# A token-parallel MLP in two passes of half the tokens, its up projection by Strassen's seven products

## The chip, the core and the metric

One core of one Trainium2 chip runs the whole inference step. The metric is the device time of one execution in microseconds (us). The kernel before takes 1367.91 us in the median of three runs (1366.85 to 1371.48).

A core has five engines that run their own instruction streams and wait for each other by semaphores: TensorE (PE; matmuls, with PEld its weight loads), VectorE (DVE), ScalarE (ACT), GpSimd (POOL) and SyncE (SP, which issues DMAs). An engine runs its instructions in order: one that waits holds up all that stand behind it.

## The reference

The step is one layer of a hybrid decoder on 1032 tokens (1024 of a prompt and 8 of single-token sequences), model width 1024:

```
h    = rmsnorm(x, g1);  proj = h @ w_in
mix  = concat(pool_mixer(proj), rwkv7_mixer(proj)) @ w_out
x    = x + mix
h2   = rmsnorm(x, norm2_g)                       # x * rsqrt(mean(x*x) + eps) * g
x    = x + square(relu(h2 @ w_up)) @ w_down      # w_up 1024 x 4096, w_down 4096 x 1024
y    = rmsnorm(x, norm_f_g)
```

All of it is float32. The change touches the last three lines, and through the order of the streams the end of the line before.

## The kernel before

A float32 product is made of three fp32r matmuls. Each operand is split into a high part h, rounded to fp32r by ScalarE, and a low part l = x - h, taken by VectorE; `gemm` (line 169) then sums h·h, h·l and l·h in PSUM. Activations lie with channels on the partitions and tokens along the free axis, so that a matmul has 128x128 weights and streams up to 512 tokens. The weights are streamed from HBM in blocks of 128x512: `weights` (line 147) loads one by GpSimd's queue into wr (four buffers) and splits it into wh and wl (six each).

The tokens have three blocks: block 0 with 512, blocks 1 and 2 with 260 each. Half 0 is block 0 and half 1 is blocks 1 and 2 (520 tokens). x, the residual stream, lies in two tiles x10 and x11, loaded by `open_x1` (line 835), into which all later results are added.

Stages: the input projections, interleaved with the mixers by a table of letters (to about 560 us); the output projection of half 0 (mx of 512 columns), then of half 1 (mx of 260 columns): `mixed` (line 842) loads a piece of the mixer's output from DRAM into mr (three buffers, SyncE's queue) and splits it into mh and ml, `out_block` adds the product to x. Half 1's is in the pool `opb` (lines 915 to 927). The norm's sums of squares follow (`norm2`), and h2h and h2l are the split of x times the gain; the reciprocal root rs2 is applied after the product, in line 910.

The MLP runs over 32 feature blocks f of 128 rows of the hidden layer. `ups_of(f)` makes one: 8 k-blocks x 3 matmuls for each of the three token blocks, then line 910 (relu and rs2), 911 (square), the rounding and 913 (low part). After four feature blocks `down(g, m, b)` (line 944) adds their share of the second product to x: for each of 8 output blocks m and each token block 12 matmuls, into one of two PSUM buffers (ps_d), and one VectorE addition (line 949). Three of the four feature blocks that a group needs are made after the group before. The last group (g = 7) runs block by block and interleaves the final norm; `final` (line 966) writes the result.

The instructions' order on each engine follows from the program text, and the pools' memory: a tile that lies where an earlier pool lay is first written when the earlier one's readers are through. DMAs of one queue are issued in the order in which they stand on its engine.

Of the kernel before, what the change touches and what calls it, by code (L numbers as in the profile page):

```python
# [84 lines left out]
def _build(ctx, nc, tc, I, O, dbg):  # L85
# [793 lines left out]
    def square_sum(ps, m, c, n, acc, sq):

        act(sq if m else acc, x1s(m, c, n), AF.Square)
        if m:
            V.tensor_tensor(acc, acc, sq, op=ALU.add)
        if m == KT - 1:
            PE.matmul(ps[:, :n], ON, acc, start=True, stop=True)

    def norm2(c, n, tmp):

        for m in range(KT):
            x, h, g = x1s(m, c, n), h2[0][:, m, c:c + n], col(V_G2, m)  # L890
            act(h, x, scale=g)
            V.scalar_tensor_tensor(h2[1][:, m, c:c + n], x, g, f32(h), ALU.mult, ALU.subtract)  # L892
# [8 lines left out]
    def up(f, w, b):
        if f not in ups:
            ups[f] = [mp.tile([P, T], F32R, tag=f"u{x}", name=f"u{x}{f}", bufs=6) for x in "hl"]
        uh, ul = ups[f]
        c, n = BLK[b]
        cs = slice(c, c + n)
        ps = ps_u.tile([P, 512], F32, tag="u", name=f"up{f}_{c}")
        gemm(ps[:, :n], w, [(h2[0][:, k, cs], h2[1][:, k, cs]) for k in range(KT)])
        u = tmp(f"u{f}_{c}")[:, :n]
        V.scalar_tensor_tensor(u, ps[:, :n], 0.0, rs2[:, cs], ALU.max, ALU.mult)  # L910
        V.tensor_tensor(u, u, u, op=ALU.mult)  # L911
        act(uh[:, cs], u)
        V.tensor_tensor(ul[:, cs], u, f32(uh[:, cs]), op=ALU.subtract)
# [17 lines left out]
    tmp = lambda x, t="u": mp.tile([P, 512], F32, tag=t, name=x, bufs=3 if t == "u" else 1)  # L931
    w = weights(I["w_up"][0])
    up(0, w, 0)
    for c, n in BLK[1:]:
        norm2(c, n, tmp)
    for b in (1, 2):
        up(0, w, b)

    def ups_of(f):
        w = weights(I["w_up"][f])  # L940
        for b in range(3):
            up(f, w, b)

    def down(g, m, b, w):
        c, n = BLK[b]
        ps = ps_d.tile([P, 512], F32, tag="d", name=f"dn{g}_{m}_{b}")
        gemm(ps[:, :n], w, [(ups[4 * g + j][0][:, c:c + n], ups[4 * g + j][1][:, c:c + n]) for j in range(4)])
# [3 lines left out]
    for f in range(1, 4):
        ups_of(f)
    for g in range(7):
        ups_of(4 * g + 4)
        for m in range(KT):
            w = weights(I["w_down"][g, m])
            for b in range(3):
                down(g, m, b, w)
        for f in range(4 * g + 5, 4 * g + 8):
            ups_of(f)  # L960


    w7 = [hq.tile([P, 8, 512], F32R, tag=f"h2{x}", name=f"w7{x}") for x in "hl"]
    ws = [weights(I["w_down"][7, m], None if m < 4 else [x[:, m, :] for x in w7]) for m in range(KT)]
    pending = []
# [102 lines left out]
```

## Time and profile before

| | |
|---|---|
| median of 3 runs | 1367.91 us (1366.85 to 1371.48) |
| profiled execution | 1369.13 us, span 1367.4 us |
| mean granted TensorE clock | 0.987 |
| PE busy | 1306.5 us, 96% of the span, 9844 matmuls |
| DVE / ACT / POOL busy | 829.6 / 592.7 / 156.5 us (61%, 43%, 11%) |
| HBM read / written | 79.67 / 13.78 MB |

The span is the time from the first to the last instruction; the profiled execution's own time is 1.7 us longer. The share of an engine is an average over stages that differ: the mixers' stage up to 560 us keeps VectorE and ScalarE busy, the MLP behind it hardly. The granted clock is that of TensorE; 1.00 is 2.4 GHz and 0.50 is 1.2 GHz.

### The profile page before, as it was taken

The numbers are of one execution on the slowest core, as the hardware profiler recorded it, in microseconds if no ns is written. First come the engines' busy times: TensorE is split into PE (matmuls) and PEld (weight loads), VectorE is DVE, ScalarE is ACT, GpSimd is POOL, SyncE is SP. The second block draws the span as 40 slices with busy tenths as digits, with TensorE's granted clock in tenths as the row PEclk, the third lists the DMA queues.
The fourth block names the chain that finished last, engine by engine and source line by source line (L and its number), as shares of the span: only waits on it lengthen the run. The fifth ranks groups of instructions, "written<-read, shape, count | busy, mean of one in ns | idle before, by whom it ended". The sixth has DMA issues, their size and how long they took to land.

```text
span 1367.4 us, 24591 instructions
## 1 busy us (share of the span) xinstructions
PE 1306.5 (96%) x9844; PEld 1158.8 (85%) x9844; DVE 829.6 (61%) x1832; ACT 592.7 (43%) x1466; POOL 156.5 (11%) x306
## 2 busy tenths in 40 slices
PE   5999999999999999999999999999999999999996
PEld 5987778788777777798999999999999999999986
DVE  8887677778778656748644435445444354453447
ACT  7768777877777758526211212112111121121123
POOL 4101000210010021120010100100000100000000
PEclk9999999899999989999999999999999999999998
DMA  6323123222221244531111111111111111111103
GB/s 199 97 55 89 39 47 83 100 96 54 59 63 42 67 152 147 167 125 59 47 54 39 55 47 39 55 40 47 55 40 54 47 46 48 45 48 48 47 7 124
DMA packets 75315, 94.82 MB, mean 69 GB/s; under 512 B 46168, under 2 KB 52440, under 8 KB 75192
## 3 DMA queue, kind: packets, MB, share of 16 engines
q0 software_dynamic: 20480, 66.04, 15.1%
q1 hardware_dynamic: 53392, 25.36, 7.1%
q10 hardware_dynamic: 1328, 1.85, 0.4%
q8 instruction: 77, 1.26, 0.4%
q14 instruction: 38, 0.31, 0.1%
HBM read 79.67 MB, written 13.78 MB: 68 GB/s over the span
## 4 chain that ended last, share of the span: by engine, by line
PE 75%; ACT 9%; DVE 9%; DMA 3%; issue 2%; POOL 1%; SPq 0%; DVEq 0%; POOLq 0%; ACTq 0%
PE dn L175 26%; PE up L175 26%; PE pj L175 7%; PE mx L175 5%; ACT SV L92 2%; DVE tm L496 1%; PE sc L403 1%; PE pcs L580 1%; ACT Es L92 1%; ACT TT L92 1%; PE pcs L577 1%; DVE SV L589 1%; ACT wh L92 1%; PE pcs L573 1%; PE bkt L417 1%
## 5 line engine op out<-in xcount | busy, mean ns | idle before, releaser
L92 ACT ACTIVATE wh<-wr 128x512 fp32r<-128x512 f32 x230 | 143.8, 626 | 353.4 <-PE dn L175 276.2
L175 PE MATMUL up<-h2h,wl 128*128 128x260 f32 (+1 forms) x768 | 245.8, 320 | 0.0
L175 PE MATMUL up<-h2h,wh 128*128 128x260 f32 (+1 forms) x768 | 245.2, 320 | 0.5 <-DVE u L910 0.5
L175 PE MATMUL up<-h2l,wh 128*128 128x260 f32 (+1 forms) x768 | 245.0, 320 | 0.0
L175 PE MATMUL dn<-uh,wl 128*128 128x512 f32 (+1 forms) x720 | 231.2, 321 | 0.0
L175 PE MATMUL dn<-ul,wh 128*128 128x512 f32 (+1 forms) x720 | 230.8, 321 | 0.0
L175 PE MATMUL dn<-uh,wh 128*128 128x512 f32 (+1 forms) x720 | 230.5, 320 | 0.0
L949 DVE TENSOR_TENSOR x<-dn,x 128x260 f32<-128x260 f32 (+1 forms) x192 | 99.1, 516 | 189.8 <-PE dn L175 189.8
L175 PE MATMUL pj<-xh,wh 128*128 128x256 f32 (+1 forms) x576 | 175.3, 304 | 13.9 <-ACT wh L92 13.7
L165 DVE TENSOR_TENSOR wl<-wr,wh 128x512 fp32r<-128x512 f32 x230 | 156.5, 684 | 44.6 <-ACT wh L92 37.8
L175 PE MATMUL pj<-xh,wl 128*128 128x256 f32 (+1 forms) x576 | 171.0, 297 | 0.2 <-DVE wl L165 0.2
L175 PE MATMUL pj<-xl,wh 128*128 128x256 f32 (+1 forms) x576 | 170.5, 296 | 0.0
L175 PEld LDWEIGHTS up<-h2l,wh 128*128 128x128 f32 x768 | 144.6, 188 | 12.1 <-DVE h2l L892 0.4
L175 PEld LDWEIGHTS up<-h2h,wh 128*128 128x128 f32 x768 | 144.3, 188 | 11.6 <-DVE u L910 0.9
L175 PEld LDWEIGHTS up<-h2h,wl 128*128 128x128 f32 x768 | 144.6, 188 | 11.0
L92 ACT ACTIVATE uh<-u 128x260 fp32r<-128x260 f32 (+1 forms) x96 | 47.2, 492 | 238.6 <-DVE u L911 238.6
L175 PEld LDWEIGHTS dn<-ul,wh 128*128 128x128 f32 x720 | 135.6, 188 | 10.9 <-issue 0.2
L175 PEld LDWEIGHTS dn<-uh,wh 128*128 128x128 f32 x720 | 135.8, 189 | 10.4
L175 PEld LDWEIGHTS dn<-uh,wl 128*128 128x128 f32 x720 | 135.5, 188 | 10.6 <-issue 0.2
L175 PEld LDWEIGHTS pj<-xh,wh 128*128 128x128 f32 x576 | 111.4, 193 | 17.4 <-ACT wh L92 13.7
L910 DVE SCALAR_TENSOR_TENSOR u<-up,rs 128x260 f32<-128x260 f32 (+1 forms) x96 | 49.5, 517 | 120.9 <-PE up L175 114.3
L175 PEld LDWEIGHTS pj<-xl,wh 128*128 128x128 f32 x576 | 111.2, 193 | 2.4 <-issue 1.9
(295 smaller groups left out, 2224.3 us busy)
## 6 DMA issues: line engine op xcount, KB each, us to landing
wr<-in_w_in POOLq DMA_DIRECT2D x72, 256.0 KB, 3.1
wr<-in_w_up POOLq DMA_DIRECT2D x64, 256.0 KB, 2.8
wr<-in_w_down POOLq DMA_DIRECT2D x64, 256.0 KB, 2.9
wr<-in_w_out POOLq DMA_DIRECT2D x26, 256.0 KB, 3.1
xr<-in_xT SPq DMA_DIRECT2D x16, 256.0 KB, 3.7
mr<-mix SPq DMA_DIRECT2D x8, 260.0 KB, 3.5
x<-in_xT SPq DMA_DIRECT2D x2, 1040.0 KB, 9.1
blk<-AA SPq DMA_DIRECT2D x16, 128.0 KB, 3.3
```

Of the source, the lines that this page charges most:

```text
L92: A.activation(out, in_, func, bias=bias, scale=scale, **k)
L165: V.tensor_tensor(l[:, :w], raw[:, :w], f32(h[:, :w]), op=ALU.subtract)
L175: PE.matmul(ps, lhs, rhs, start=i == 0, stop=i == n - 1)
L403: PE.matmul(psc[:, c, :], BK[:, c, 2 * h:2 * h + 2, :], AR[:, c, :, h, :], start=True, stop=True)
L417: PE.transpose(pt[:, c, :], BK[:, c, 2 * h:2 * h + 2, :].rearrange("p a t -> p (a t)"), ident)
L496: V.tensor_tensor(pr[:, q], l[:, q].unsqueeze(2).to_broadcast([64, m, m, m]), r[:, q].rearrange("p k j -> p j k").unsqueeze(1).to_broadcas ...
L573: PE.matmul(pq, AR[:, c, 0, :, :], SV[:, c, :, :], start=True, stop=True)
L577: PE.matmul(pa, TT[:, g, :, :], Q, start=True, stop=True)
L580: PE.matmul(pu, BKT[:, c, :, :], SV[:, c, :, :], start=True, stop=True)
L589: V.scalar_tensor_tensor(dst, pu[R[h], h, :], U.gam[R[h], g:g + 1], sg[R[h], h, :], ALU.mult, ALU.add)
L910: V.scalar_tensor_tensor(u, ps[:, :n], 0.0, rs2[:, cs], ALU.max, ALU.mult)
L949: V.tensor_tensor(d, ps[:, :n], d, op=ALU.add)
```

## The change

The MLP runs in two passes: all 32 feature blocks of half 0, then all of half 1. In each pass the up projection takes the feature blocks in pairs, and a pair's product (256 features x 1024 channels by 1024 channels x 512 or 520 tokens) is cut into quarters: two feature blocks, two halves of the channels, two quarters of the tokens (q = 256 or 260). Of the eight products of quarters, Strassen's scheme (in Winograd's form) makes seven, of sums and differences of quarters:

- `up_operands(half)` makes the seven token operands x11, xt2, x21, xt3, xt1, x22, xt4: for each of four k-blocks four normed quarters b11 to b22 (x times gain times rs2, so that the norm is applied ahead of the product), four differences, and the split of seven. That is 60 VectorE and 28 ScalarE instructions a half. Its tiles have one buffer each (x11 two), so half 1's overwrite half 0's.
- `up_pair(p)`, p = 0 to 31, loads the four weight quarters a11 to a22 (128x512, SyncE's queue, one buffer each), makes four sums s1 to s4 on GpSimd, splits seven operands, and runs 7 products of 12 matmuls of q columns, b0 to b6; seven VectorE sums put the four results together, and `emit` does relu, square and rounding on ScalarE and the low part on VectorE.
- w_up and w_down are read twice; w_down's blocks come by SyncE's queue instead of GpSimd's.
- A down group of half 0 has 8 blocks of 512 columns, of half 1 8 x 2 of 260. The order on TensorE is pair 0, 1, 2, group 0, pair 3, 4, group 1, and so on; `up_operands(1)` stands ahead of group 7 of half 0, pair 16 and 17 behind it, then block 0's final norm.

The core of the diff:

```diff
-    def weights(src, into=None):
+    def weights(src, into=None, q=GP):
...
-                GP.dma_start(raw[:, :w], src[:, o:o + w])
+                q.dma_start(raw[:, :w], src[:, o:o + w])
...
+    def split(raw):
+
+        h = wp.tile([P, 512], F32R, tag="wh", name="wh", bufs=NWH)
+        l = wp.tile([P, 512], F32R, tag="wl", name="wl", bufs=NWH)
+        act(h, raw)
+        V.tensor_tensor(l, raw, f32(h), op=ALU.subtract)
+        return h, l
...
+    def up_operands(half):
+
+        c0, n = HALF[half]
+        q = n // 2
+        for i in KIND:
+            XO[half][i] = [hq.tile([P, 4, 260], F32R, tag=f"x{i}{x}", name=f"x{i}{x}{half}", bufs=NXO[i]) for x in "hl"]
...
+        for k in range(4):
+            b = {}
+            for i, (kk, o) in {"11": (k, c0), "12": (k, c0 + q), "22": (k + 4, c0 + q), "21": (k + 4, c0)}.items():
+                b[i] = xtmp(f"b{i}_{k}_{half}", q)
+                V.scalar_tensor_tensor(b[i], x1s(kk, o, q), col(V_G2, kk), rs2[:, o:o + q], ALU.mult, ALU.mult)
+            for out, x, y in (("t1", "12", "11"), ("t2", "22", "t1"), ("t3", "22", "12"), ("t4", "21", "t2")):
+                b[out] = b["12"] if out == "t3" else xtmp(f"{out}_{k}_{half}", q)
+                V.tensor_tensor(b[out], b[x], b[y], op=ALU.subtract)
+            for i in KIND:
+                put(i, k, b[i])
...
+    def up_pair(p):
+
+        half, f0 = p // 16, 2 * (p % 16)
+        q = HALF[half][1] // 2
+        X = XO[half]
...
+                a[i] = mp.tile([P, 512], F32, tag=f"a{i}", name=f"a{i}_{p}")
+                SY.dma_start(a[i], I["w_up"][f0 + f][:, 512 * k:512 * k + 512])
+        for out, x, y, op in (("s3", "11", "21", ALU.subtract), ("s1", "21", "22", ALU.add), ("s2", "s1", "11", ALU.subtract),
+                              ("s4", "12", "s2", ALU.subtract)):
+            a[out] = mp.tile([P, 512], F32, tag=f"a{out}", name=f"a{out}_{p}")
+            GP.tensor_tensor(a[out], a[x], a[y], op=op)
...
+        def product(s, x):
+            i = next(banks)
+            ps = (ps_u if i % 3 else ps_m).tile([P, 512], F32, tag="u" if i % 3 else "m", name=f"b{i}_{p}")[:, :q]
+            h, l = split(a[s])
+            for k in range(4):
+                c = slice(P * k, P * k + P)
+                xh, xl = (t[:, k, :q] for t in X[x])
+                for i, (lhs, rhs) in enumerate(((h, xh), (h, xl), (l, xh))):
+                    PE.matmul(ps, lhs[:, c], rhs, start=k == i == 0, stop=k == 3 and i == 2)
+            return ps
...
+        ps = product("11", "11")
+        p1 = tmp("p1")
+        act(p1, ps)
+        u2 = plus("u2", p1, product("s2", "t2"))
+        emit(0, 0, plus("c11", p1, product("12", "21")))
+        u3 = plus("u3", u2, product("s3", "t3"))
+        ps = product("s1", "t1")
+        u4 = plus("u4", u2, ps)
+        emit(1, 1, plus("c22", u3, ps))
+        emit(1, 0, plus("c21", u3, product("22", "t4")))
+        emit(0, 1, plus("c12", u4, product("s4", "22")))
...
         norm2(0, 512, lambda x: op.tile([P, 512], F32, tag="n2", name=x, bufs=2))
+        up_operands(0)
...
+    up_pair(0)
+    for c, n in BLK[1:]:
+        norm2(c, n, tmp)
+    up_pair(1)
+    for G in range(15):
+        half, g = G // 8, G % 8
+        if G != 7:
+            up_pair(2 * G + 2)
+        else:
+            up_operands(1)
+        for m in range(KT):
+            w = weights(I["w_down"][g, m], q=SY)
+            for blk in MB[half]:
+                down(g, m, blk, w)
+        if G == 7:
+            up_pair(2 * G + 2)
+        up_pair(2 * G + 3)
```

How the order of the streams stands before and after is shown at three places. The first is SyncE's queue at the output projection of half 1; x11 is half 1's residual tile, mr its mixer pieces. Before:

```order
L698 DMA mix7_1_85<-da_6384 128x8
L849 DMA mr0_1_7148<-mix0_1_71 128x520
L849 DMA mr1_1_7154<-mix1_1_73 128x520
L849 DMA mr2_1_7160<-mix2_1_75 128x520
L849 DMA mr3_1_7166<-mix3_1_77 128x520
L849 DMA mr4_1_7172<-mix4_1_79 128x520
L849 DMA mr5_1_7178<-mix5_1_81 128x520
L849 DMA mr6_1_7184<-mix6_1_83 128x520
L849 DMA mr7_1_7703<-mix7_1_85 128x520
L835 DMA x11_7127<-in_xT 128x4x520 x2
```

And now, with the first loads of the MLP behind them:

```order
L709 DMA mix7_1_85<-da_6384 128x8
L846 DMA x11_7127<-in_xT 128x4x520 x2
L860 DMA mr0_1_7146<-mix0_1_71 128x520
L860 DMA mr1_1_7152<-mix1_1_73 128x520
L860 DMA mr2_1_7158<-mix2_1_75 128x520
L860 DMA mr3_1_7164<-mix3_1_77 128x520
L860 DMA mr4_1_7170<-mix4_1_79 128x520
L860 DMA mr5_1_7176<-mix5_1_81 128x520
L860 DMA mr6_1_7182<-mix6_1_83 128x520
L860 DMA mr7_1_7815<-mix7_1_85 128x520
```

The two loads of x11, which wait for half 0's last matmul in both kernels, stand ahead of the eight mr loads now.

The second is VectorE at a change from ups to a down group, group 4 of half 0 (dn4_0 is its first block, wl the low part of a weight block, u and ul those of the hidden layer). Before:

```order
L165 TENSOR_TENSOR wl_11818<-wr_11815,wh_11817 128x512
L910 SCALAR_TENSOR_TENSOR u20_772_11618<-up20_772_11593,rs2_7141 128x260
L911 TENSOR_TENSOR u20_772_11618<-u20_772_11618 128x260
L165 TENSOR_TENSOR wl_11866<-wr_11863,wh_11865 128x512
L913 TENSOR_TENSOR ul20_11532<-u20_772_11618,uh20_11531 128x260
L949 TENSOR_TENSOR x10_6590<-dn4_0_0_11629,x10_6590 128x512
L949 TENSOR_TENSOR x11_7127<-dn4_0_1_11643,x11_7127 128x260
```

And now (wr_10628 is the group's fifth block, c21 and c12 are a pair's last two results):

```order
L168 TENSOR_TENSOR wl_10611<-wr_10608,wh_10610 128x512
L974 TENSOR_TENSOR c21_10_10517<-u3_10_10472,b5_10_10500 128x256
L168 TENSOR_TENSOR wl_10631<-wr_10628,wh_10630 128x512
L970 TENSOR_TENSOR ul21_10376<-u11_10_10495,uh21_10375 128x256
L974 TENSOR_TENSOR c12_10_10541<-u4_10_10491,b6_10_10524 128x256
L168 TENSOR_TENSOR wl_10651<-wr_10648,wh_10650 128x512
L970 TENSOR_TENSOR ul21_10376<-u10_10_10519,uh21_10375 128x256
L970 TENSOR_TENSOR ul20_10374<-u01_10_10543,uh20_10373 128x256
L1016 TENSOR_TENSOR x10_6590<-dn4_0_0_10554,x10_6590 128x512
L168 TENSOR_TENSOR wl_10671<-wr_10668,wh_10670 128x512
L1016 TENSOR_TENSOR x10_6590<-dn4_1_0_10574,x10_6590 128x512
```

The low parts of six of the group's blocks now stand ahead of its first addition; on SyncE the load of wr_10628 stands behind the loads of the next pair and the first of the one after:

```order
L160 DMA wr_10608<-in_w_down 128x512
L942 DMA a11_10_10377<-in_w_up 128x512
L942 DMA a12_10_10381<-in_w_up 128x512
L942 DMA a22_10_10383<-in_w_up 128x512
L942 DMA a21_11_10714<-in_w_up 128x512
L942 DMA a11_11_10712<-in_w_up 128x512
L942 DMA a12_11_10716<-in_w_up 128x512
L942 DMA a22_11_10718<-in_w_up 128x512
L942 DMA a21_12_10889<-in_w_up 128x512
L160 DMA wr_10628<-in_w_down 128x512
```

Before, these loads were on GpSimd's queue in the order of their use.

The third is VectorE at the change from half 0 to half 1 (l1 ends the name of an operand of half 1, dn7_0 is the first block of half 0's last group). Before, the same addition stands among the low parts of u and the final norm; now:

```order
L924 TENSOR_TENSOR t4_3_1_12017<-b21_3_1_12010,t2_3_1_12014 128x260
L915 TENSOR_TENSOR xt2l1_11906<-t2_3_1_12014,xt2h1_11905 128x260
L915 TENSOR_TENSOR x21l1_11908<-b21_3_1_12010,x21h1_11907 128x260
L915 TENSOR_TENSOR xt3l1_11910<-b12_3_1_12006,xt3h1_11909 128x260
L915 TENSOR_TENSOR xt1l1_11912<-t1_3_1_12012,xt1h1_11911 128x260
L915 TENSOR_TENSOR x22l1_11914<-b22_3_1_12008,x22h1_11913 128x260
L915 TENSOR_TENSOR xt4l1_11916<-t4_3_1_12017,xt4h1_11915 128x260
L1016 TENSOR_TENSOR x10_6590<-dn7_0_0_12039,x10_6590 128x512
L1016 TENSOR_TENSOR x10_6590<-dn7_1_0_12059,x10_6590 128x512
```

The last operands of half 1 stand ahead of the first addition of the group.

## Rows read from the trace of the kernel before

**Rows 1.** Busy time by stretches: us, busy PE, PEld, DVE, ACT, POOL, clock, DMA, GB/s
```profile
700.00:900.00 200.00, 200.00 (x1275) 181.52 (x1275) 90.25 (x166) 34.47 (x60) 18.80 (x35) 1.00 0.15 47
1100.00:1300.00 200.00, 200.00 (x1271) 181.26 (x1270) 92.78 (x172) 36.92 (x65) 19.35 (x36) 1.00 0.16 48
```

**Rows 2.** Timeline of PE in a down group: start us, us, engine, line
```profile
800.16 0.28 PE L175 MATMUL dn<-uh,wh 128*128 128x260 f32 x1
...
802.93 0.28 PE L175 MATMUL dn<-uh,wl 128*128 128x260 f32 x1
803.05 0.39 PE L175 MATMUL dn<-uh,wh 128*128 128x512 f32 x1
...
805.59 0.39 PE L175 MATMUL dn<-uh,wl 128*128 128x512 f32 x1
```

**Rows 3.** Timeline of PE in an input projection
```profile
289.13 0.28 PE L175 MATMUL pj<-xh,wh 128*128 128x256 f32 x1
...
291.87 0.28 PE L175 MATMUL pj<-xh,wl 128*128 128x256 f32 x1
```

**Rows 4.** Timeline of DVE in the output projection of half 1
```profile
587.58 0.69 DVE L165 TENSOR_TENSOR wl<-wr,wh 128x512 fp32r<-128x512 f32 x1 [1.54 <-ACT wh L92]
588.18 0.42 DVE L860 TENSOR_TENSOR x<-mx,x 128x260 f32<-128x260 f32 x1
588.54 0.56 DVE L165 TENSOR_TENSOR wl<-wr,wh 128x384 fp32r<-128x384 f32 x1
```

**Rows 5.** Groups of instructions from 640 us on: count, busy us and mean ns, idle before
```profile
L92 ACT ACTIVATE wh<-wr 128x512 fp32r<-128x512 f32 x117 | 74.1, 633 | 300.7 <-PE dn L175 276.2 <-PE up L175 24.2
...
L971 DVE SCALAR_TENSOR_TENSOR x<-x,vec,rs 128x512 f32<-128x512 f32 x8 | 5.8, 746 | 0.0
```

**Rows 6.** Timeline of SP's issues at the output projection
```profile
563.14 11.22 SPq L849 DMA_DIRECT2D mr<-mix  x8
574.40 0.98 SPq L835 DMA_DIRECT2D x<-in_xT  x2
```

**Rows 7.** DMA issues of the page: count, KB each, us to landing
```profile
wr<-in_w_down POOLq DMA_DIRECT2D x64, 256.0 KB, 2.9
...
xr<-in_xT SPq DMA_DIRECT2D x16, 256.0 KB, 3.7
mr<-mix SPq DMA_DIRECT2D x8, 260.0 KB, 3.5
...
glu<-in_g_lora_up SPq DMA_DIRECT2D x1, 256.0 KB, 8.9
```

**Rows 8.** Tile x, 574 to 590 us: its two loads from issue to landing
```profile
DMA to landing us min/median/max: 7.9/9.1/10.4
```

**Rows 9.** The chain that ended last, half 1's output projection: start us, us
```profile
582.77 35.42 PE mx L175 x294
```

**Rows 10.** Timeline of PE at the MLP's start, in brackets the idle time before
```profile
646.02 0.70 PE L885 MATMUL ss<-acc,cst 128*128 128x260 f32 x2 [0.74 <-DVE acc L883]
647.25 0.39 PE L175 MATMUL up<-h2h,wh 128*128 128x260 f32 x1 [0.52 <-DVE u L910]
```

**Rows 11.** Groups of instructions on POOL
```profile
L434 POOL MEMSET RB<- 128x512 f32 x4 | 1.9, 522 | 0.0
```

**Rows 12.** Timeline of PE, two matmuls behind a gap (its us in brackets)
```profile
244.92 0.80 PE L577 MATMUL pcs<-Q,TT 128*128 128x128 f32 x2 [2.90 <-ACT Q L92]
...
582.77 0.39 PE L175 MATMUL mx<-mh,wh 128*128 128x260 f32 x1 [2.37 <-DVE x L860]
```

**Rows 13.** Stretches behind three gaps, as in rows 1 (clock ahead of the DMA share)
```profile
245.00:251.00 6.00, 6.00 (x21) 5.31 (x22) 2.82 (x7) 4.67 (x14) 3.22 (x6) 0.50 0.60 201
490.00:500.90 10.90, 10.90 (x90) 7.98 (x88) 6.22 (x11) 5.54 (x14) 2.13 (x4) 0.53 0.41 137
583.00:587.00 4.00, 4.00 (x35) 4.00 (x35) 2.24 (x5) 0.72 (x2) 0.54 (x1) 1.00 0.62 221
```

More of the change, by code (lines that the diff above doesn't have):

```diff
@@ L38 @@
 NX = 2
+NXT = 8
+NUT = 10
+NXO = {"11": 2, "t2": 1, "21": 1, "t3": 1, "t1": 1, "22": 1, "t4": 1}
 QUEUE = 1
@@ L875, in _build @@
     hq = open_pool(ctx, "h2", reuse_waits="tile")
-    h2 = [hq.tile([P, KT, T], F32R, tag=f"h2{x}", name=f"h2{x}") for x in "hl"]
+    KIND = ("11", "t2", "21", "t3", "t1", "22", "t4")
+    XO = [{}, {}]
     rs2 = hq.tile([P, T], F32, name="rs2")
[L879 to L885, printed above, removed]
+    xtmp = lambda x, n: hq.tile([P, 260], F32, tag="xt", name=x, bufs=NXT)[:, :n]
     def norm2(c, n, tmp):
[L889 to L892, printed above, removed]
         ss = ps_m.tile([P, 512], F32, tag="m", name=f"ss2{c}")
@@ L895, in norm2 @@
         for m in range(KT):
-            square_sum(ss, m, c, n, acc, m and tmp(f"sq2_{c}_{m}")[:, :n])
-        rstd(rs2[:, c:c + n], ss[:, :n], tmp(f"ms2{c}")[:, :n], tmp(f"tt2{c}")[:, :n])
-    ups = {}
[L901 to L913, printed above, removed]
+            sq = tmp(f"sq2_{c}_{m}")[:, :n] if m else acc
@@ new lines, in norm2, with put @@
+            act(sq, x1s(m, c, n), AF.Square)
+            if m:
+                V.tensor_tensor(acc, acc, sq, op=ALU.add)
+        PE.matmul(ss[:, :n], ON, acc, start=True, stop=True)
+        rstd(rs2[:, c:c + n], ss[:, :n], tmp(f"ms2{c}")[:, :n], tmp(f"tt2{c}")[:, :n])
+    def up_operands(half):
[3 more added lines that the diff above has]
+            XO[half][i] = [hq.tile([P, 4, 260], F32R, tag=f"x{i}{x}", name=f"x{i}{x}{half}", bufs=NXO[i]) for x in "hl"]
+        def put(i, k, x):
+            h, l = (t[:, k, :q] for t in XO[half][i])
+            act(h, x)
+            V.tensor_tensor(l, x, f32(h), op=ALU.subtract)
+        for k in range(4):
[8 more added lines that the diff above has]
+                put(i, k, b[i])
@@ L930, in _build, with down @@
     mp = open_pool(ctx, "mlp", reuse_waits="tile")
[L931 to L947, printed above, removed]
+    tmp = lambda x, t="u": mp.tile([P, 512], F32, tag="v" + t, name=x, bufs=2 if t == "u" else 1)
+    MB = [[BLK[0]], BLK[1:]]
+    def down(g, m, blk, w):
+        c, n = blk
+        half = int(c > 0)
+        o = c - 512 * half
+        ps = ps_d.tile([P, 512], F32, tag="d", name=f"dn{g}_{m}_{c}")
+        gemm(ps[:, :n], w, [tuple(t[:, o:o + n] for t in ups[32 * half + 4 * g + j]) for j in range(4)])
         d = x1s(m, c, n)
         V.tensor_tensor(d, ps[:, :n], d, op=ALU.add)
[L951 to L965, printed above, removed]
     def final(b, m, rs):
@@ L975, in final, with final_scale @@
             (A if m == 3 else SY).dma_start(O["yT"][:, m + 1 - k:m + 1, c:c + n], x1[h][:, m + 1 - k:m + 1, o:o + n])
-    for b, (c, n) in enumerate(BLK):
+    def final_scale(b, ss):
+        c, n = BLK[b]
+        rs = mp.tile([P, 512], F32, tag="rs3", name=f"rs3{b}", bufs=2)[:, :n]
+        rstd(rs, ss[:, :n], tmp(f"ms3{b}")[:, :n], tmp(f"tt3{b}")[:, :n])
+        return [(b, m, rs) for m in range(KT)]
+    up_pair(0)
[15 more added lines that the diff above has]
+        up_pair(2 * G + 3)
+        if G == 7:
+            c, n = BLK[0]
+            ss = ps_m.tile([P, 512], F32, tag="m", name="ss30")
+            acc = tmp("acc30", "acc")
+            for m in range(KT):
+                sq = tmp(f"sq3_0_{m}") if m else acc
+                act(sq, x1s(m, c, n), AF.Square)
+                if m:
+                    V.tensor_tensor(acc, acc, sq, op=ALU.add)
+            PE.matmul(ss, ON, acc, start=True, stop=True)
+            for x in final_scale(0, ss):
+                final(*x)
+    w7 = [[hq.tile([P, 4, 260], F32R, tag=f"x{i}{x}", name=f"w7{i}{x}", bufs=NXO[i]).rearrange("p k t -> p (k t)")[:, :512]
+           for x in "hl"] for i in KIND[:4]]
+    ws = [weights(I["w_down"][7, m], None if m < 4 else w7[m - 4], q=SY) for m in range(KT)]
+    pending = []
+    for b in (1, 2):
+        c, n = BLK[b]
         ss = ps_u.tile([P, 512], F32, tag="u", name=f"ss3{b}")
@@ L980, in _build @@
         for m in range(KT):
-            down(7, m, b, ws[m])
+            down(7, m, BLK[b], ws[m])
             d = x1s(m, c, n)
@@ L994, in _build @@
             pending = []
-        rs = mp.tile([P, 512], F32, tag="rs3", name=f"rs3{b}", bufs=2)[:, :n]
-        rstd(rs, ss[:, :n], tmp(f"ms3{b}")[:, :n], tmp(f"tt3{b}")[:, :n])
-        pending += [(b, m, rs) for m in range(KT)]
+        pending += final_scale(b, ss)
     for q in pending:
```

22 lines of the change are left out of this document (21 added, 1 removed).

## The prediction

> **What bounds the kernel now.** I read the table of busy time by stretches first, since the page's shares mix the mixer's many small stages with the MLP. From 700 to 1300 us TensorE is busy in every microsecond at the full granted clock, while VectorE stands at 45% and the rings carry 47 to 48 GB/s [rows 1]: the MLP is bound by TensorE's columns and nothing else. A change that takes matmuls away there gains their pace in full, and a change that makes TensorE wait pays in full too. The second view was the timeline, for the pace from start to start (the busy time of a matmul overlaps the next one's): eleven steps of 128x512 from 803.05 to 805.59 give 0.231 us each, 23 steps of 128x260 from 800.16 to 802.93 give 0.120 [rows 2], 23 steps of 128x256 from 289.13 to 291.87 give 0.119 [rows 3].
>
> **The matmuls.** Before, the up projection is 32 x (24 x 0.231 + 48 x 0.120) = 362 us. After, it is 32 pairs of 7 products of 12 matmuls: 1344 of 256 columns and 1344 of 260, 1344 x (0.119 + 0.120) = 322 us. That is -40.4 us. The down projection has the same matmuls in another order. That seven eighths are paid for is certain; the question is what else TensorE now waits for. A pair lasts 84 x 0.119 = 10.0 us, a down group of half 0 (8 blocks of 12 matmuls of 512 columns) 96 x 0.231 = 22.2 us, so a period of two pairs and a group is 42.2 us in half 0 and 43.3 in half 1.
>
> **Bulk work beside it.** VectorE's paces are 0.60 for 128x512 (587.58 to 588.18) and 0.36 or less for 128x260 (588.18 to 588.54) [rows 4]; I use 0.61 and 0.35. Per pair: 7 lower parts of weights, 7 sums, 4 lower parts of u: 7 x 0.61 + 11 x 0.35 = 8.1 us; a down group adds 8 lower parts and 8 additions, 9.8 us; together 26 of 42.2. ScalarE, by busy means [rows 5], is lower still. So neither becomes the bound on average. The second reading of both weights adds 33.5 MB over about 700 us, 48 GB/s, where the rings are 15% busy [rows 1]: nothing by itself. The 64 more splits of w_down are in the 26.
>
> **Places where TensorE waits.**
>
> 1, out-projection of half 1. Before, SyncE issues the eight mr loads from 563.14 on, and the two loads of x for half 1 behind them at 574.40 [rows 6], when half 0's last matmul lets them. After, the order has x first and the mr loads behind. The x loads take 7.9 and 10.4 us to land [rows 8], an mr load 3.5 [rows 7]; behind 2 MB on the same queue, mr0 lands at about 586, and with three buffers for eight loads, each to be rounded and subtracted before the next is issued, the seventh is split at about 597. The matmuls that began at 582.77 [rows 9] begin at 597.5: +14.7. If the rings serve both loads side by side it is +7; if every mr load takes its 3.5 behind the other, +18. I take 14.7, since a 256 KB load behind others on this queue took 8.9 [rows 7]. The 35.4 us of matmuls behind [rows 9] cover the 60 operand instructions of half 0 on VectorE (60 x 0.35 = 21 us).
>
> 2, start of the MLP. The a tiles lie over the out-projection's memory, so a11's load is issued when the last of its matmuls ends. A 256 KB load on this queue takes 3.7 [rows 7], three more follow at 0.6 each (2.5 us lie between the landings of the two x loads of 1040 KB [rows 8]). Then s1 and s2 on GpSimd, one behind the other, then the rounding, 0.63 [rows 5]: the second product starts at 3.7 + 1.8 + 2.4 + 0.6, some 9 us behind, of which the first has filled 1.4: +8. Norm sums of blocks 1 and 2 share pairs 0 to 2 with 8.1 us of VectorE per pair: +2.5. The idle times of before at this place, 0.74 and 0.52 [rows 10], go: -1.3.
>
> 3, every period. VectorE's order has the lower part of w_down's fifth block ahead of the first addition of a group. Its load stands on SyncE behind the a21 load two pairs on, which waits until GpSimd has read a21 for s1, which waits for a22, which can be loaded only when the pair before has split its own. From the end of a group: 3.5 for a22, two GpSimd sums, the split in the next pair, again 3.5 and two sums, and 2.9 for the block [rows 7] land it about 21.5 us into the period, where the group starts at 20.0; with two PSUM buffers its third block is late by some 1.4. Seven periods of half 0 at 1.4 and seven of half 1 at 0.3 make +12. A GpSimd sum of 128x512 does not occur before; the nearest row is a MEMSET of that size, 0.52 [rows 11], one stream where the sum has three, so 0.5 to 1.6. I take 1.2, in the upper half because of the two reads. At 0.5 the term is 0, at 1.6 about 35.
>
> The Trainium skill (GPSIMD Engine Reference, 3.1 Elementwise) has 4497 ns for such a sum of 2048 columns, an estimate of 1.1 us here; by that the term would stay at 12.
>
> 4, middle. The operand tiles of half 0 are single, so half 1's are written when pair 15 has read them. On VectorE all 32 instructions of k = 2 and 3 stand ahead of the addition of dn7_0. They take 32 x 0.35 = 11 us and some 5 for the turns with ScalarE's roundings, from pair 15's end at 10.0: about 26. TensorE has two PSUM buffers to go on with, for dn7_0 and dn7_1, until 10.0 + 2 x 2.8 = 15.6. It then idles: +10.3.
>
> 5, small ones. Block 0's eight final products (0.75 busy each [rows 5]) stand ahead of the lower parts for the next group: +2.4; the end: +0.5.
>
> 6, clock. After TensorE's gap of 2.9 us that ends at 244.92 [rows 12] the granted clock stood at 0.50, its 1.2 GHz level, for the 6 us that follow, and from 490 on at 0.53 for 10.9 us; the gap of 2.37 before 582.77 [rows 12] left it at 1.00, 2.4 GHz [rows 13]. Half of 6.0 is a loss of 3.0, 0.47 of 10.9 one of 5.1, and the third is none. Places 1, 2 and 4 have gaps three to five times longer, so I take 3.3 for each: +9.9, bounds 0 and 15.
>
> Sum: -40.4 + 14.7 + 8.0 + 2.5 - 1.3 + 12.0 + 10.3 + 2.4 + 0.5 + 9.9 = +18.6. The profiled execution of before took 1369.1 (span 1367.4), 1.2 above the median of 1367.9; I set the sum on the median: 1386.5, forecast 1387, own range 1374 to 1404.
>
> **Rivals.**
>
> A, SyncE's loads land sooner than I priced them. Places 1 to 3 hang on loads of one queue, and their rows were taken beside others. If mr is served beside x, place 1 is +7 and its gap short enough to spare the clock, as at 583; if a 256 KB load takes 2 us in the quiet MLP, place 2 is +6.5, and a block of w_down lands 3 us earlier, which ends place 3. Only the middle, which waits for no load, keeps its clock loss: -40.4 + 7 + 6.5 + 2.5 - 1.3 + 0 + 10.3 + 2.4 + 0.5 + 3.3 = -9.2, 1359. It decides from a load under some 2.5 us. For it: the rings are 15% busy in the MLP [rows 1]. Against: there w_down's loads take 2.9 by the other queue [rows 7]. With place 1 at nothing it would be 1352; the matmuls alone would give 1328. Chance 0.19.
>
> B, they cancel: between A and the forecast, loads of 2.7, place 1 at 10 and place 3 at 5, one clock loss: -40.4 + 10 + 8 + 2.5 - 1.3 + 5 + 10.3 + 2.4 + 0.5 + 3.3 = 0, 1368. Chance 0.10.
>
> C, GpSimd and VectorE get in each other's way, so that GpSimd's 4 x 1.2 us per pair add to VectorE's 8.1: 12.9 against 10.0 of TensorE. Within a period the first pair can draw on the group before it, the second cannot: 16 x 2.9 = 46 in place of 12, +53, 1420. It decides when a sum is over about 0.5 us in such exclusion. Before has no GpSimd instruction in the MLP that reads memory but load issues, so no row speaks for or against. Chance 0.14.
>
> The Trainium skill (SBUF — State Buffer, Who interferes with whom) says that a VectorE instruction with two inputs in SBUF contends with a GpSimd instruction that reads SBUF, and that one then waits for the other's end. All lower parts have two such inputs, the sums with PSUM one; by that rule rival C is the mechanism; no run here shows it.
>
> **How the numbers follow.** Forecast 0.57, A 0.19, B 0.10, C 0.14. The range leaves out the lower part of A and the upper part of C: 1354 to 1422. Faster by over 0.3% (4 us, what a measurement of this kernel can tell): A and a little of B, 0.21; within 0.3%: 0.08; slower: 0.71.
>
> **What would show it.** In the profile after: 2688 up matmuls at 0.12 us; the first matmul of half 1's out-projection near 597 with the mr loads issued behind x; gaps of about 8 us before pair 0's second product and of 10 before dn7_2; a clock of 0.50 after them; stalls of about 1.4 before dn_2 in half 0, released by the lower part of w_down. If the GpSimd sums last over 2 us or the gaps come at every product inside pairs, it is C; if the steady periods of half 0 last 42.2 us and the place 1 gap is under 8, it is A. I am wrong if the order of the queues is not what sets the time, that is if TensorE's idle time lies elsewhere than in places 1 to 4.

## The result, and the profile after

The changed kernel takes 1445.45 us in the median of four runs (1443.41 to 1446.36), the kernel before 1367.38 beside it: ratio 1.057, interval 1.0544 to 1.0596. Slower was forecast, at 1387 with a range to 1422; it is 23 us above that. The profiled execution has a span of 1444.4 us, 77 more than before, and a mean clock of 0.956.

Busy time by stretches of the kernel after, in steady periods of half 0 and of half 1 (columns as in [rows 1], which has TensorE busy throughout):

```profile
690.00:960.00 270.00, 256.98 (x1575) 227.81 (x1574) 185.62 (x318) 130.83 (x287) 67.75 (x48) 0.99 0.30 94
1100.00:1300.00 200.00, 187.63 (x1506) 186.92 (x1505) 133.61 (x249) 89.08 (x195) 46.34 (x33) 0.97 0.28 86
1231.40:1279.30 47.90, 45.03 (x361) 44.85 (x361) 32.00 (x60) 21.81 (x49) 11.36 (x8) 0.96 0.28 87
```

TensorE now idles 5 to 6% of the steady time, and the clock drops in every period of half 1 and in two of the six of half 0. No engine beside TensorE is near full: VectorE is at 69 and 67%. Where TensorE waits, by its timeline (in brackets the idle time before and who ended it):

```profile
586.64 0.58 PE L186 MATMUL mx<-mh,wh 128*128 128x260 f32 x1 [10.34 <-ACT mh L95]
...
646.66 0.58 PE L959 MATMUL b<-x11h,wh 128*128 128x256 f32 x1 [3.47 <-ACT wh L95]
652.35 0.58 PE L959 MATMUL b<-xt2h,wh 128*128 128x256 f32 x1 [2.46 <-ACT wh L95]
679.52 0.80 PE L902 MATMUL ss<-acc,cst 128*128 128x260 f32 x1 [7.39 <-DVE acc L901]
...
885.02 0.47 PE L186 MATMUL dn<-uh,wh 128*128 128x512 f32 x1 [2.34 <-DVE x L1016]
1023.00 0.79 PE L186 MATMUL dn<-uh,wh 128*128 128x512 f32 x1 [7.11 <-DVE x L1016]
1279.27 0.41 PE L186 MATMUL dn<-uh,wh 128*128 128x260 f32 x1 [2.87 <-DVE x L1016]
```

The first answers to [rows 9], the next three are the MLP's start, 885 and 1279 are two of twelve such gaps (one a full period, 2.3 to 3.8 us), 1023 is the middle. At 646 and 652 TensorE waits for ScalarE's rounding of a weight, which waits for the pair's first load and then for GpSimd's sums (the third ends at 651.6). In the gaps shown from 679 on it waits for VectorE. Why VectorE is late is in its own rows and GpSimd's, here in the second pair of a period of half 0:

```profile
873.11 0.69 DVE L168 TENSOR_TENSOR wl<-wr,wh 128x512 fp32r<-128x512 f32 x1
...
874.05 1.45 DVE L168 TENSOR_TENSOR wl<-wr,wh 128x512 fp32r<-128x512 f32 x1
875.42 0.41 DVE L974 TENSOR_TENSOR u<-u,b 128x256 f32<-128x256 f32 x1
875.75 1.45 DVE L168 TENSOR_TENSOR wl<-wr,wh 128x512 fp32r<-128x512 f32 x1
877.13 1.51 DVE L970 TENSOR_TENSOR ul<-u,uh 128x256 fp32r<-128x256 f32 x1
...
883.85 0.42 DVE L970 TENSOR_TENSOR ul<-u,uh 128x256 fp32r<-128x256 f32 x1 [0.77 <-ACT uh L95]
884.19 0.68 DVE L1016 TENSOR_TENSOR x<-dn,x 128x512 f32<-128x512 f32 x1
```

```profile
861.00 1.29 POOL L946 TENSOR_TENSOR as<-a,a 128x512 f32<-128x512 f32 x1 [6.99 <-DVE wl L177]
...
873.41 1.53 POOL L946 TENSOR_TENSOR as<-a,a 128x512 f32<-128x512 f32 x1 [3.55 <-DMA a<-in_w_up]
875.03 1.63 POOL L946 TENSOR_TENSOR as<-as,a 128x512 f32<-128x512 f32 x1
876.73 1.62 POOL L946 TENSOR_TENSOR as<-a,as 128x512 f32<-128x512 f32 x1
```

While GpSimd makes a sum (873.4 to 878.3), VectorE's instructions with both operands in SBUF last 1.45 to 1.51 us instead of 0.69 and 0.42: each ends 0.3 to 0.6 us behind the end of a sum. Those with an operand in PSUM (u<-u,b) keep their 0.41, and ScalarE's roundings of the sums take 627 ns in the mean, where roundings of weights took 626 before, so not everything that reads SBUF is slower. In this stretch VectorE loses 2.6 us, the addition that frees TensorE's PSUM buffer comes at 884.19, and TensorE goes on at 885.02. The groups over the MLP (mean ns behind the busy time), VectorE's and then GpSimd's:

```profile
L168 DVE TENSOR_TENSOR wl<-wr,wh 128x512 fp32r<-128x512 f32 x124 | 101.1, 818 | 7.7 <-ACT wh L95 4.9
L177 DVE TENSOR_TENSOR wl<-as,wh 128x512 fp32r<-128x512 f32 x128 | 100.7, 792 | 53.2 <-ACT wh L95 50.7
...
L970 DVE TENSOR_TENSOR ul<-u,uh 128x256 fp32r<-128x256 f32 x64 | 39.6, 618 | 5.6 <-ACT uh L95 4.7
```

```profile
L946 POOL TENSOR_TENSOR as<-a,a 128x512 f32<-128x512 f32 x64 | 90.5, 1415 | 567.0 <-DVE wl L177 378.8
```

A sum takes 1.42 us, near the upper bound of 1.6 got from [rows 11] (at 861.00, with VectorE idle for most of it, 1.29). VectorE also stands idle 53.2 us ahead of the lower parts of sums (wl<-as), which it takes in order. The split of w_down (L168) waits for hardly anything, 7.7 us in the whole MLP: the prediction's third place is not what these rows show.

### The profile page after: what moved, and what is told of

The parts are those of the page before. It is cut to its first block, busy times and chain, and to the rows that moved or that the text cites. A ratio compares the mean times of both kernels' runs of the same rounds, so it can differ in the third digit from the quotient of the medians.

```text
span 1444.4 us, 27213 instructions
## 1 busy us (share of the span) xinstructions
PE 1305.1 (90%) x10226; PEld 1178.7 (82%) x10226; DVE 1041.6 (72%) x2217; ACT 824.8 (57%) x2042; POOL 269.1 (19%) x306
## 3 DMA queue, kind: packets, MB, share of 16 engines
q10 hardware_dynamic: 1328, 1.85, 0.4%
## 4 chain that ended last, share of the span: by engine, by line
PE 54%; DVE 18%; ACT 16%; issue 5%; DMA 5%; POOL 2%; DVEq 0%; POOLq 0%; SPq 0%; ACTq 0%
PE dn L186 22%; PE b L959 9%; PE pj L186 7%; PE mx L186 6%; ACT wh L95 3%; POOL as L946 2%; DMA a<-in_w_up 2%; ACT SV L95 2%; DVE wl L177 1%; DVE tm L507 1%; DVE wl L168 1%; DVE ul L970 1%; ACT c L95 1%; DMA wr<-in_w_down 1%; PE pcs L591 1%
## 5 line engine op out<-in xcount | busy, mean ns | idle before, releaser
L186 PE MATMUL dn<-uh,wh 128*128 128x260 f32 (+1 forms) x736 | 246.1, 335 | 44.7 <-DVE x L1016 40.7
L186 PE MATMUL dn<-uh,wl 128*128 128x260 f32 (+1 forms) x736 | 244.3, 332 | 4.7 <-DVE wl L168 4.7
L186 PE MATMUL dn<-ul,wh 128*128 128x260 f32 (+1 forms) x736 | 244.1, 332 | 0.0
L946 POOL TENSOR_TENSOR as<-a,a 128x512 f32<-128x512 f32 x64 | 90.5, 1415 | 567.0 <-DVE wl L177 378.8
L168 DVE TENSOR_TENSOR wl<-wr,wh 128x512 fp32r<-128x512 f32 x230 | 172.1, 753 | 32.3 <-ACT wh L95 25.3
L186 PE MATMUL pj<-xh,wh 128*128 128x256 f32 (+1 forms) x576 | 174.7, 303 | 13.7 <-ACT wh L95 13.6
L95 ACT ACTIVATE wh<-as 128x512 fp32r<-128x512 f32 x128 | 79.3, 627 | 148.2 <-PE dn L186 97.4
L177 DVE TENSOR_TENSOR wl<-as,wh 128x512 fp32r<-128x512 f32 x128 | 100.7, 792 | 53.2 <-ACT wh L95 50.7
L186 PEld LDWEIGHTS pj<-xh,wh 128*128 128x128 f32 x576 | 110.9, 193 | 16.9 <-ACT wh L95 13.6
L95 ACT ACTIVATE wh<-a 128x512 fp32r<-128x512 f32 x96 | 60.1, 626 | 106.4 <-PE dn L186 98.3
L186 PEld LDWEIGHTS pj<-xh,wl 128*128 128x128 f32 x576 | 110.7, 192 | 1.6 <-issue 0.7
L95 ACT ACTIVATE c<-c 128x256 f32<-128x256 f32 (+1 forms) x128 | 52.7, 412 | 77.7 <-DVE c L974 77.0
L970 DVE TENSOR_TENSOR ul<-u,uh 128x256 fp32r<-128x256 f32 (+1 forms) x128 | 74.6, 583 | 8.7 <-ACT uh L95 7.7
```

Source lines behind the costliest of these rows:

```text
L95: A.activation(out, in_, func, bias=bias, scale=scale, **k)
L177: V.tensor_tensor(l, raw, f32(h), op=ALU.subtract)
L186: PE.matmul(ps, lhs, rhs, start=i == 0, stop=i == n - 1)
L946: GP.tensor_tensor(a[out], a[x], a[y], op=op)
L970: V.tensor_tensor(ul, u, f32(uh), op=ALU.subtract)
```

## The experiments

The theory after the result, G: GpSimd's sums read SBUF and so hold up VectorE's instructions with two SBUF operands (and VectorE waits for the sums too). The rival, W, is the prediction's place 3: w_down's loads stand behind those of the a tiles on SyncE's queue. Each run is timed beside the kernel before.

**1, no sums on GpSimd.** The sums are left out, `product` splits a quarter:

```diff
-            GP.tensor_tensor(a[out], a[x], a[y], op=op)
...
-            h, l = split(a[s])
+            h, l = split(a[{"s2": "11", "s3": "21", "s1": "12", "s4": "22"}.get(s, s)])
```

> GpSimd makes no sums of weight quarters; the products that used them take a quarter itself in their place, so the up projection's values are others. Theory G (GpSimd's sums make VectorE late: it waits in order for a sum of the next pair, and its own instructions are stretched beside them): periods fall from 45.1 to about 42.2 us in half 0 and from 47.9 to about 43.3 in half 1, the 2.4 to 2.9 us stalls before a group's third block go, and the whole falls by 45 to 55 us, to about 1395. Theory W (w_down's fifth block stands behind the loads of the a tiles): the block comes earlier by two sums of 1.4 us, so this one alone would fall too, to about 1400; the next run tells them apart.

1369.24 us, ratio 1.0021 (0.9996 to 1.0046). That is 76 us below the changed kernel, and no clear difference from the kernel before is left: more than expected. From one down group to the next it is 42.1 us in half 0 and 43.3 in half 1 (its first period apart, 46.5), TensorE's pace as forecast. The same two stretches as above, and the lower parts of the pairs' weights:

```profile
690.00:960.00 270.00, 270.00 (x1672) 241.69 (x1672) 174.75 (x327) 138.99 (x296) 0.00 (x0) 1.00 0.35 98
1100.00:1300.00 200.00, 200.00 (x1667) 200.00 (x1666) 140.89 (x284) 109.12 (x235) 0.00 (x0) 1.00 0.36 102
```

```profile
L177 DVE TENSOR_TENSOR wl<-a,wh 128x512 fp32r<-128x512 f32 x224 | 153.6, 688 | 30.8 <-ACT wh L95 22.4
```

**2, sums made and not used.** Only the `split` line of run 1 is changed; GpSimd works as after the change.

> GpSimd makes all sums as after the change, but no product uses them (the products take the quarters as in the run without sums). Theory G in its port form (VectorE's instructions are slowed beside GpSimd's): stretched instructions remain, a stall of 0.5 to 1.5 us a period remains, 1405 to 1420. Theory G in its waiting form (VectorE waits for a sum): all stalls gone, within 4 us of the run without sums. Theory W: the a21 tile is still freed by GpSimd's sum, so w_down's block is as late as after the change, 1440 to 1446.

1433.24 us, ratio 1.0476 (1.0432 to 1.0521). With no product waiting for a sum, only 12 us go; 64 of the 76 stay. The time alone does not tell G from W: it lies between their forecasts (1405 to 1420, and 1440 to 1446), and the a tiles are still freed by the sums. VectorE's instructions tell more. Its groups, then GpSimd's first:

```profile
L177 DVE TENSOR_TENSOR wl<-a,wh 128x512 fp32r<-128x512 f32 x224 | 190.8, 854 | 24.6 <-ACT wh L95 16.0
L168 DVE TENSOR_TENSOR wl<-wr,wh 128x512 fp32r<-128x512 f32 x124 | 105.8, 856 | 3.5 <-ACT wh L95 1.0
```

```profile
L946 POOL TENSOR_TENSOR as<-a,a 128x512 f32<-128x512 f32 x64 | 87.2, 1362 | 559.7 <-DMA a<-in_w_up 559.7
```

The same two groups of run 1 have 688 and 687 ns. So VectorE is held up beside the sums though it waits for none of them, the port form of G, and its size was set too low in the expectation.

**3, sums on VectorE.** `V.tensor_tensor` in place of `GP.tensor_tensor`; everything is computed.

> The four sums of a pair are made by VectorE. Theory G: VectorE gets 4 x 0.61 = 2.4 us more work a pair, 10.5 against TensorE's 10.0, but no stretching and sums of 0.6 in place of 1.4 us; the stalls shrink to 1 or less, about 1400 to 1415. If VectorE's own load is what makes it late, the stalls grow to 4 or more and the time is over 1460. Theory W: the chain to w_down's block is shorter by 1.6, stalls of about 1, 1420.

1381.84 us, ratio 1.0101 (1.0023 to 1.0178): 64 us less than after the change, though VectorE has 128 instructions more.

```profile
690.00:960.00 270.00, 270.00 (x1660) 241.19 (x1660) 203.61 (x388) 138.14 (x300) 0.00 (x0) 1.00 0.34 100
1100.00:1300.00 200.00, 199.97 (x1660) 199.34 (x1659) 153.54 (x311) 102.52 (x220) 0.00 (x0) 1.00 0.32 94
```

VectorE is busier than after the change (203.6 of 270, against 185.6) and TensorE waits for nothing. Its 75% is no bound. That the stalls would only shrink was too careful.

**4, norm late.** `norm2` for blocks 1 and 2 is moved from between pairs 0 and 1 to group 3.

> The sums of squares of half 1 (blocks 1 and 2) are taken before group 3 of half 0 and not between pair 0 and pair 1; nothing needs them before half 1. Theory S (at the start TensorE waits in order for the norm's matmul, whose sums stand behind pair 0 on VectorE): the gap of 7.4 us and the half clock behind it go, 1445 falls by 8 to 14 us to about 1434. Rival: pairs 0 to 2 are late anyway because their weights come late, so the gap moves to the products: within 4 us of 1445.

1442.57 us, ratio 1.0545 (1.0499 to 1.0590): 3 us, the rival's time but not for its reason. The gap of 7.39 is gone, and from the end of the projection to the first down group it is 43.5 us instead of 53.8, as theory S has it. But from there to group 7 it is 316.3 instead of 307.3: 6 of the 9 us are lost in the period of group 3, where the norm's work stands now and new gaps of 1.2, 1.2 and 0.6 us appear. The work was moved from one stall into another.

**5, GpSimd only writes.** Run 1, and at the end of each pair:

```diff
+        for _ in range(11):
+            GP.memset(a["21"], 0.0)
```

> As the run without sums, but GpSimd clears the a21 tile eleven times a pair, 11 x 0.52 = 5.7 us of writes, as long as four sums, with nothing read; the up projection's values are others. If VectorE is slowed by what GpSimd reads, its 128x512 lower parts stay at 0.69 us and its 128x256 ones at 0.43, and the time stays within 10 us of 1369. If any work of GpSimd slows it (writes, or the shared memory as a whole), they stand at 0.8 and 0.6 as with sums and the time is 1415 to 1435.

1369.5 us, ratio 1.0021 (1.0007 to 1.0035), as run 1. GpSimd is as busy as with sums, and VectorE is not touched:

```profile
L988 POOL MEMSET a<- 128x512 f32 x352 | 185.3, 526 | 525.0 <-DVE wl L177 506.6
```

```profile
L177 DVE TENSOR_TENSOR wl<-a,wh 128x512 fp32r<-128x512 f32 x224 | 153.8, 689 | 31.3 <-ACT wh L95 22.8
L168 DVE TENSOR_TENSOR wl<-wr,wh 128x512 fp32r<-128x512 f32 x124 | 85.0, 689 | 11.5 <-ACT wh L95 7.4
```

So it is what GpSimd reads, not that it works or writes. The run speaks against W too, but less sharply: a21 is freed later than in run 1 here as well and the periods are 42.1 and 43.3, yet w_down's loads are issued 4.1 us ahead of their group (888.2 for 892.3), after the change only 1.6 (875.4 for 877.0).

**10, two sums on GpSimd** (s3 and s4; s1 and s2 on VectorE).

> Of a pair's four sums GpSimd makes s3 and s4 and VectorE s1 and s2, else as after the change. If GpSimd's reading slows VectorE in proportion, the lower parts of 128x512 stand between 0.69 and 0.82 us and the time half way between 1382 and 1445, at 1400 to 1420. If only the chain of sums through s1 and s2 that VectorE waits for matters, 1380 to 1390.

1395.69 us, ratio 1.0216 (1.0181 to 1.0251). The lower parts of 128x512 stand at 0.86 and 0.80 us, about as long as with four sums, but the time is 14 above run 3, not the 32 of half way: half 0's periods are 42.1, and only half 1's, at 44.8, are late. Less than in proportion: VectorE has slack to lose before TensorE waits.

**11, w_down on another queue.** Kernel after, `q=A` (ScalarE's queue) in place of `q=SY` for w_down.

> As after the change, but the blocks of w_down are loaded by ScalarE's queue, so that they no longer stand behind the loads of the a tiles on SyncE's. Theory W (the step of the prediction: this queue makes the groups late): periods fall to about 42.2 and 43.3 us and the time to about 1390 to 1400. Theory G (GpSimd's reading slows VectorE, which is late whatever the queue): periods stay within 1 us of 45.1 and 47.9 and the time at 1436 to 1452.

1415.22 us, ratio 1.0344 (1.0322 to 1.0366): 30 us less, between the two theories. The order of VectorE's stream changes with the queue; at the period's end it now reads

```profile
866.99 0.68 DVE L168 TENSOR_TENSOR wl<-wr,wh 128x512 fp32r<-128x512 f32 x1
867.59 0.68 DVE L1016 TENSOR_TENSOR x<-dn,x 128x512 f32<-128x512 f32 x1
868.19 0.41 DVE L970 TENSOR_TENSOR ul<-u,uh 128x256 fp32r<-128x256 f32 x1
```

The first addition stands ahead of the pair's last two low parts, where after the change it stood behind them (883.85 and 884.19 above, with a wait for ScalarE). Half 0's periods are 42.5 to 42.8 and half 1's 45.3 to 47.0, the first of each apart; VectorE's lower parts are as slow as after the change (861 and 797 ns). So beside GpSimd's sums the queue, or the order that it changes, is worth 30 us. Run 3 leaves w_down on SyncE's queue and has no stall in its steady periods, but its loads are earlier too (4.5 us ahead of their group), so it does not show that the queue is worth nothing by itself. How much is the queue and how much the moved addition stays open.

**6, mr ahead of x.** From here on with the sums on VectorE (1382 us). mr has seven buffers, and x11 is loaded behind the pieces:

```diff
-    open_x1(1)
+    open_x1(1, False)
...
-        ops = [mixed(op, k, 1, 3) for k in range(KT - 1)]
+        ops = [mixed(op, k, 1, 7) for k in range(KT - 1)]
+        load_x1(1)
```

> Sums on VectorE (1382 us), and half 1's mr tiles have seven buffers and are loaded ahead of the two loads of x. Theory Q (the two loads of x ahead in the queue are the 10 us gap at half 1's output projection and its slow pace behind): the gap falls to about 2.4 as before the change and the whole to 1366 to 1371. Rival: the pieces then wait for x as the last addition's operand, as before, and the gap only moves: 1376 to 1382.

1395.5 us, ratio 1.0206 (1.0174 to 1.0238): slower than run 3 and above both forecasts. The gap did fall, from 10.3 to 3.3, but another came ahead of the projection's last products:

```profile
579.38 0.78 PE L186 MATMUL mx<-mh,wh 128*128 128x260 f32 x2 [3.33 <-ACT mh L95]
...
650.88 0.59 PE L186 MATMUL mx<-mh,wh 128*128 128x260 f32 x1 [20.74 <-DVE x L876]
```

On VectorE the norm of half 0 (L138) starts at 626.51 and its operands (L926) at 629.32: TensorE's matmul for the norm comes at 623.24 now, late in the projection, where in run 3 it comes at 582.25, just behind the gap; and the last additions stand behind the operands (650.40). The prediction held these 21 us to be covered; they are only while the projection is late.

**7, operands of half 1 between the blocks.** `up_operands` yields after each k; k = 2 and 3 are made behind the third and fifth block of group 7.

> Sums on VectorE (1382 us), and half 1's operands for k = 2 and 3 are made between the blocks of half 0's last down group (behind the third and the fifth) and not ahead of all its additions. Theory M (the gap of 9.4 us is VectorE's order): the gap and the half clock behind it go and TensorE runs on: 1367 to 1373. Rival: the operands are the bound themselves, so that TensorE waits as long before pair 16: 1378 to 1384.

1378.33 us, ratio 1.0077 (1.0050 to 1.0104). 3.5 us below run 3, within the spread of the runs (1374.44 to 1381.37 here) and at the rival's number: the gap of 9.4 is gone, but what stands in its place is 0.3, 2.2 and 1.6 in the group and 1.6 and 4.3 in the pairs behind it:

```profile
982.44 0.51 PE L186 MATMUL dn<-uh,wh 128*128 128x512 f32 x1 [0.32 <-DVE x L1017]
985.41 0.77 PE L186 MATMUL dn<-uh,wl 128*128 128x512 f32 x1 [2.24 <-DVE wl L168]
994.96 0.50 PE L186 MATMUL dn<-uh,wl 128*128 128x512 f32 x1 [1.56 <-DVE wl L168]
```

**8, all of it.** Runs 3, 6 and 7 together, half 1's norm in groups 1 to 4, pair 0's a tiles in wr buffers, block 0's final products in a later group.

> All of it: sums on VectorE; mr ahead of x; operands of half 1 between the blocks of group 7; pair 0's weight quarters in buffers that are free early; the norm sums of half 1 taken in groups 1 to 4, their matmul a group behind; block 0's final products spread over a later group. If the gaps are separate, 1382 - 13 - 12 - 16 (start) - 5 = about 1336, faster than before by 2.3%; with the matmuls alone it would be 1328. If TensorE's waits only move, 1355 to 1370.

1374.64 us, ratio 1.0050 (1.0028 to 1.0071). A miss, for run 6's reason: from 628 to 648 TensorE waits again and again for half 0's operands.

**9 and 12, all of it, with the operands dealt out.** In 9 half 0's norm is emitted behind the second block of the projection and its operands behind four more, and block 0's final norm goes to groups 8 to 10; in 12 the operands of both halves come in eight steps:

```diff
+            if m == 1:
+                next(early), next(early)
+            if m > 1:
+                next(first)
...
+            if G == 7 and m in (1, 3, 4, 6):
+                next(later)
```

> As the run with all of it, but half 0's norm matmul and operands stand between the blocks of half 1's output projection in the program, and not behind all of them, so that VectorE can make them under its matmuls; block 0's final norm moves from group 7 to groups 8 to 10. Theory O (in the run with all of it, the operands of half 0 started at 629 because their norm's matmul stood behind the whole projection, 21 us of VectorE with TensorE idle): the stretch from 627 to 657 shrinks by 18 to 25 us and the whole to 1345 to 1355, faster than before by 1 to 1.6%. Rival: VectorE cannot do both under the projection, and the additions to x come late: 1362 to 1372.

> As the second run with all of it, but the operands of both halves are dealt out in eight smaller steps between the blocks, so that VectorE's additions and lower parts of weights stand behind 7 or 8 of its instructions and not 15. If the remaining gaps (0.7, 5.4 and 1.2 us at half 0's operands, 2.3 and 1.6 at half 1's) come from that, 1357 falls by 6 to 12 us to about 1348; if VectorE's sum of work there is what counts, 1354 to 1359.

Run 9: 1357.4 us, ratio 0.9944 (0.9923 to 0.9965), between its two forecasts. Run 12: 1348.69 us, ratio 0.9859 (0.9840 to 0.9877), as forecast, faster than before by 1.4%. Its first gaps:

```profile
575.38 0.80 PE L186 MATMUL mx<-mh,wh 128*128 128x260 f32 x2 [3.33 <-ACT mh L95]
584.88 0.39 PE L186 MATMUL mx<-mh,wh 128*128 128x260 f32 x1 [1.43 <-DVE x L876]
```

No later gap is over 3.4 us. 1349 is 21 above the 1328 that the matmuls alone would give.

## Why the prediction was wrong

**The matmuls, right.** Without GpSimd's sums the periods are 42.1 and 43.3 us, against 42.2 and 43.3 worked out. The 40.4 us were saved, and more was lost in waits. (1344 x 0.239 is 321, not 322; the difference stands.)

**Place 1, right in mechanism.** The two rows of SyncE after the change, answering to [rows 6]:

```profile
576.09 0.93 SPq L846 DMA_DIRECT2D x<-in_xT  x2
577.07 12.02 SPq L860 DMA_DIRECT2D mr<-mix  x6
```

The first mr load lands 8.9 us behind its issue, at 586.0, as forecast. Half 1's projection ends at 643.2, 67.1 behind the issue of x, of which its 384 matmuls need 46.2: 20.9 lost. Before, it ended 54.6 behind, with 19 matmuls of the up projection in it (4.4 us): 4.0 lost. That is +16.9, where 14.7 and 3.3 of clock were forecast. The way there was another one: the matmuls began earlier (586.64, not 597.5) but went slowly, 56 of them in the 13.4 us to 600, at a clock of 0.76.

**Places 2 and 4, right in place, low in size.** From 643.2 to the first down group at 697.0 the three pairs take 53.8 us for 31.2 of matmuls: +21.3 against before, where 12.5 was forecast (8.0 + 2.5 - 1.3 and 3.3 of clock). From group 7 of half 0 to the first of half 1 it is 74.5 for 53.0: +21.5, forecast 13.6 with its clock. In run 1 both are 9 us shorter; that is GpSimd's part, and what is left, 12 and 13, is near the forecast. At the start this is in part luck. The terms that the prediction adds for place 2 give 8.5 and not some 9, it counts two sums ahead of the second product where three are made (s3 is first), and run 1 makes none; the longest gap is the 7.39 us ahead of the norm's matmul (6.40 in run 1), for which it had 2.5. In the middle, two k-blocks are 30 instructions of VectorE, not 32.

**Place 3, the step that failed.** Forecast +12, as a late load of w_down, with nothing for what GpSimd's sums do to VectorE. (At a sum of 1.1 us, the estimate that it names, its own working gives about 7 and not 12.) The periods lost 21.9 us in half 0 and 35.4 in half 1: +57. Of these, 4.7 us, the gap ahead of 1084.09, are place 5's: the eight final products stand ahead of w_down's lower part there, for which 2.4 was forecast. The stall came where it was said, ahead of a group's third block, but VectorE was hardly waiting for w_down (7.7 us in all); it was late because GpSimd's reading had held it up, by 2.6 us ahead of the gap of 2.34 that is shown above. Added up, -40.4 + 16.9 + 21.3 + 57.3 + 21.5 = +76.6, of the 77 us between the two profiled spans.

That is rival C, which had 0.14 and a price of +53 on the whole, 1420. C had the mechanism, but its price is 25 us short: it put 46 us on the periods and nothing on the start and the middle, while by run 1 the sums cost 55 in the periods and 18 in the other two. Nor do the two engines' times simply add, as C reckoned: in run 2, 184 us of sums lengthen VectorE's busy time by 80. Runs 2 and 5 show the mechanism: 64 of the 76 us stay when no product waits for a sum, and nothing stays when GpSimd writes and does not read. What part of the time w_down's queue has beside it (run 11) is open.

The rule of the Trainium skill weighed beside rival C (SBUF — State Buffer, Who interferes with whom) says that VectorE's instructions with two inputs in SBUF contend with those of GpSimd that read SBUF, and not with those that only write it; runs 1, 2 and 5 agree, with 0.69 us alone, 0.85 beside sums and 0.69 beside clears. The prediction gave it 0.14 because no row of before could show it. It should have had more: the kernel before has no reading GpSimd instruction in the MLP, so its trace could not speak against the rule either.

**The clock, right in kind.** It fell behind places 1, 2 and 4 (0.76 from 586.6 to 600, 0.56 from 643.1 to 655, 0.72 from 1023 to 1030) and, not foreseen, in each period of half 1 (0.96 from 1231.4 to 1279.3, some 1.7 us a period) and in two of half 0. The prediction took the length of the gap for what decides it; among gaps as short as these it does not (last section).

Without place 3 the prediction's sum is +6.6; run 1, which is the change without GpSimd's sums, measured +1.5; place 2's price holds two sums that run 1 does not make.

## What to carry to other kernels

An idle engine is not free: before giving GpSimd elementwise work, see what VectorE does in the same time, and if its instructions read two operands from SBUF, count part of GpSimd's time as VectorE's (80 of 184 us here). Test such a cost by making the work and using it nowhere, and by work that writes only. And when an operation is moved out of a stall, look for what had been hidden under the stall (runs 6 and 8), and for whether the place it moves to is one itself (run 4).

## What the runs showed of the hardware that was not expected

- GpSimd's sums of 184 us made VectorE's busy time longer by 80 us (1069.6 against 989.5 in the pages of runs 2 and 1); GpSimd's clears of 185 us by 0.2 (989.7 in run 5).
- Both sides pay: a sum takes 1.29 us with no VectorE instruction on two SBUF operands beside it (861.00), and 1.53 to 1.63 among them (873 to 878).
- Gaps of one length went with either clock: in half 0 the 7 us behind gaps of 2.38 and 2.34 us (at 748.36 and 885.02) have 1.00, those behind 2.37 and 2.32 (793.33 and 930.12) 0.74 and 0.75. In half 1 every period has such a gap, 2.8 us or more, and a mean of 0.96 or 0.97 (0.93 in the first). In run 11, with gaps of 1.8 to 2.0, its periods have 1.00 and 0.96 by turns.
